# Three output blocks' share of one hidden block moved from TensorE to VectorE, and the low parts of the weights from VectorE to GpSimd

## The chip, the core and the metric

The kernel runs on one core of one Trainium2 chip. A core has TensorE (PE, the matrix unit, which writes to the PSUM banks only), VectorE (DVE), ScalarE (ACT), GpSimd (POOL), SyncE (SP, which here issues nearly all transfers) and 16 DMA engines that all transfers share. Every engine works through its own instructions strictly in their written order; semaphores tie the engines together. The metric is the device time of one execution in microseconds (us), the median of several runs.

## What is computed

The model is one step of a small decoder layer on T = 288 tokens (256 new ones of one prompt and 8 x 4 of samples). What matters here is the last part, the MLP with a width of 8192:

```python
h2 = rmsnorm(x, norm2_g)
f = jnp.square(jax.nn.relu(jnp.einsum("btd,df->btf", h2, w_ff1)))   # 2048 -> 8192
x = x + jnp.einsum("btf,fd->btd", f, w_ff2)                         # 8192 -> 2048
```

Everything before it (a norm, a projection, a convolution group, a pooling group, an output projection `w_out`) takes the first quarter of the time. Inputs, weights and outputs are float32.

## The kernel before

Activations lie transposed, channels on the 128 partitions and the 288 tokens in the free dimension; `xT` holds the residual stream as 16 blocks of 128 channels. TensorE works on rounded 32-bit numbers, so each operand is split into a high part (a cast on ScalarE) and a low part (the difference, a subtraction), and one product of a 128x128 weight block with a 128x288 activation block is three matmuls: high x high, high x low, low x high (`product`, L288 to L293). The three add into the same PSUM bank.

The MLP goes in four chunks of 2048 hidden channels (`FCH`). A chunk has a first half (FF1: 8 groups of two blocks, each summed over the 16 blocks of `xT`) and a second (FF2: 8 groups of two output blocks, each summed over the chunk's 16 hidden blocks). A group is thus 16 x 2 products, 96 matmuls (`gemm`). It goes over the 16 blocks, and inside each over its two PSUM banks, so two banks are in use at a time. There are four such banks (`acc`, bufs=4), so the next group has two banks while the last one's are read out. Two further pools of two banks each (`cvp`, `msp`) serve other uses.

- FF1's read-out: VectorE takes relu and the scale `r2` in one instruction (L584, tile `t`), ScalarE squares (`f`) and casts (`fh`), VectorE subtracts (`fl`, L589).
- FF2's read-out: VectorE adds the bank to `xT` (L600, the function `evict`).
- Weights come as tiles of 128x1024 (`wr`, 512 KB each, six buffers), four to a group. ScalarE casts each to `whi` (L284), and VectorE (GpSimd in the first stages) subtracts to `wlo` (L285). There are four buffers of each, so a tile's cast waits until TensorE has done with the tile four before it. The generator `weight_groups` decides which engine makes which low part; the split of a group stands one group ahead of its matmuls.

The order on each engine is set by a scheduler at build time, which gives each piece of work a place by its estimate of when it can run, work inside `later()` behind all other that is ready. Data dependencies follow the order in which the Python text issues the work: of two instructions that write the same slice of `xT`, the one issued first in the text stays first. When it places a group it also picks the banks, so a bank that is held long is simply not there for the groups after it.

In the stage before the MLP (`w_out`, two halves of 8 groups) the convolution's norm lies between the halves: a token sum (`pt`, L227), a few small VectorE instructions, a transposition back (`pr`, L276), then `n`, `cc`, `mh` per block, and the second half's matmuls read `mh`.

Of the kernel before, what the change touches and what calls it, by code (L numbers as in the profile page):

```python
# [9 lines left out]
F32 = mybir.dt.float32  # L10
F32R = mybir.dt.float32r
AF = mybir.ActivationFunctionType
ALU = mybir.AluOpType
# [3 lines left out]
P = 128  # L17
# [3 lines left out]
T = SEQ + NB * NS  # L21
DC = DP = 1024
DFF = 8192
# [6 lines left out]
N8 = DC // P  # L30
WINDOWS = (2, 4, 8, 16)
FCH = 2048
US = CH + NS
UO = CH + SEQ
UL = UO + NB * US
ZS = PH + NS
# [5 lines left out]

GROUPS = (3, 2, 1, 0)
SEQUENCE = [("conv", i) for i in range(2, 7)] + [("pool", 3), ("pool", 2), ("pool", 1), ("mix", 3), ("pool", 0), ("mix", 2), ("conv", 7)]


def weight_blocks():

    def w_in(*cols):
        return [("w_in", r, cols) for r in range(0, D, 1024)]  # L50

    a, b = [w_in(i * P, DC + i * P) for i in range(2)]
    yield from (a[0], b[0], a[1], b[1])
    for kind, i in SEQUENCE:
        if kind == "mix":
            if i == 3:
                yield "pool_w", 0, (0, P)
            continue
        yield from w_in(i * P, DC + i * P) if kind == "conv" else w_in(2 * DC + 2 * i * P, 2 * DC + (2 * i + 1) * P)
    for r in (DC, 0):  # L60
        for c in range(0, D, 256):
            yield "w_out", r, (c, c + P)
    for ch in range(0, DFF, FCH):
        for c in range(ch, ch + FCH, 256):
            for r in range(0, D, 1024):
                yield "w_ff1", r, (c, c + P)
        for c in range(0, D, 256):
            for r in range(ch, ch + FCH, 1024):
                yield "w_ff2", r, (c, c + P)
# [12 lines left out]
def trunk_kernel(ctx: ExitStack, tc: tile.TileContext, io):  # L82
    nc = tc.nc
# [5 lines left out]
    actp = ctx.enter_context(tc.tile_pool(name="actp", bufs=40))  # L89
    tmpp = ctx.enter_context(tc.tile_pool(name="tmpp", bufs=6))  # L90
    prdp = ctx.enter_context(tc.tile_pool(name="prdp", bufs=1))
    acc = ctx.enter_context(tc.tile_pool(name="acc", bufs=4, space=PSUM))
    cvp = ctx.enter_context(tc.tile_pool(name="cvp", bufs=2, space=PSUM))
    msp = ctx.enter_context(tc.tile_pool(name="msp", bufs=2, space=PSUM))
# [3 lines left out]
    def nm(s):  # L98
        seen[s] = seen.get(s, 0) + 1
        return f"{s}{seen[s]}"  # L100

    @contextmanager
    def later(by=LATER):

        tc.cur_priority += by
        yield
        tc.cur_priority -= by

    def row(name):
        return rowp.tile([P, T], F32, name=nm(name), tag="row")  # L110
# [4 lines left out]
    def act(name, **kw):  # L115
        return slot(name, F32R, **(kw or {"tag": "act"}))
# [13 lines left out]
    def f32(t):  # L130
        return t[:].bitcast(F32)
# [8 lines left out]
    xT = const.tile([P, KT, T], F32, name="xT")  # L140
    uz = const.tile([P, N8 * (UL + ZL)], F32, name="uz")
# [137 lines left out]
    def split(raw, eng, cuts=((0, 4),)):  # L279

        hi = wspl.tile([P, 4, 256], F32R, name=nm("whi"), tag="whi")
        lo = wspl.tile([P, 4, 256], F32R, name=nm("wlo"), tag="wlo")
        for a, b in cuts:
            nc.scalar.copy(hi[:, a:b, :], raw[:, a:b, :])  # L284
            eng.tensor_tensor(lo[:, a:b, :], raw[:, a:b, :], hi[:, a:b, :].bitcast(F32), op=ALU.subtract)  # L285
        return hi, lo

    def product(bank, rhs, w, first, last):  # L288

        (xh, xl), (wh, wl), b = rhs, w, bank[:, :T]  # L290
        nc.tensor.matmul(b, wh, xh, start=first, stop=False)  # L291
        nc.tensor.matmul(b, wh, xl, start=False, stop=False)  # L292
        nc.tensor.matmul(b, wl, xh, start=False, stop=last)  # L293

    def gemm(banks, rhs, m_outer=False, hooks={}):

        n = len(rhs)
        get = ready.pop()
        order = [(k, m) for k in range(n) for m in range(len(banks))]
        if m_outer:  # L300
            order.sort(key=lambda km: km[1])
        for j, (k, m) in enumerate(order):
            hooks.get(j, bool)()
            product(banks[m], rhs[k], get(k, m), k == 0, k == n - 1)
        ready.extend(itertools.islice(weights, 1))

    korder = [2 * g + m for g in GROUPS for m in range(2)]
# [1 line left out]
    def halves(parts, at=lambda k: k):  # L309

        def get(k, m):
            k = at(k)
            return tuple(t[:, k % 4, m * P : (m + 1) * P] for t in parts[k // 4])

        return get

    def weight_groups():

        V, G = nc.vector, nc.gpsimd
        def mix(g):  # L320

            return halves(parts, lambda k: 2 * g + k)

        for kind, i in SEQUENCE:
            if kind == "mix":
                if i == 3:
                    parts = [split(raw, G) for raw in load()]
                yield mix(i)
            else:
                yield halves([split(raw, G) for _ in range(2) for raw in load()])  # L330
        yield mix(1)
        yield mix(0)
        for _ in range(8):
            yield halves([split(raw, G) for raw in load()], lambda k: korder[k])
        for _ in range(8):
            yield halves([split(raw, V) for raw in load()])
        for _ in range(2 * DFF // 256):
            yield halves([split(raw, V) for _ in range(2) for raw in load()])

    weights = weight_groups()  # L340
    ready = []
# [15 lines left out]
    for c in range(8):  # L357
# [5 lines left out]
        for k0, k1 in steps:  # L363
# [174 lines left out]
    for g in range(8):  # L538
        bk = bank2()
# [10 lines left out]
    for g in range(8):  # L550
        bk = bank2()
        gemm(bk, mixc)
        for m in range(2):
            k = 2 * g + m
# [9 lines left out]
            else:  # L564
                q2 = bank("q", cvp, "cv")[:, :T]
                nc.scalar.activation(q2, xk, AF.Square)
                nc.vector.tensor_tensor(ss2, ss2, q2, op=ALU.add)

    r2 = row("r2")
    ss2 = parts(ss2)  # L570
    pss = ms("pss")
# [2 lines left out]
    pf = ms("pf", 8)  # L574
    for ch in range(DFF // FCH):
        fx = []
        for g in range(FCH // 256):
            bk = bank2()
            gemm(bk, x1, hooks={4: lambda: column_sum(pss, ones_r, ss2)} if ch == 0 and g == 0 else {})
            if ch == 0 and g == 0:  # L580
                rsqrt_wide(pss, r2, 1.0 / D)
            for m in range(2):
                t = tmp("t")
                nc.vector.scalar_tensor_tensor(out=t, in0=bk[m][:, :T], scalar=0.0, in1=r2, op0=ALU.max, op1=ALU.mult)  # L584
                f = tmp("f")
                nc.scalar.activation(f, t, AF.Square)
                fh, fl = act("fh"), act("fl")
                nc.scalar.copy(fh, f)
                nc.vector.tensor_tensor(fl, f, f32(fh), op=ALU.subtract)  # L589
                fx.append((fh, fl))  # L590
        last = ch == DFF // FCH - 1
        for g in range(8):
            bk = bank2()

            def evict(m):

                nonlocal last_square
                k = 2 * g + m
                xk = xT[:, k, :]
                nc.vector.tensor_tensor(xk, xk, bk[m][:, :T], op=ALU.add)  # L600
                if last:
                    if k == 0:
                        nc.scalar.activation(ssf, xk, AF.Square)
                    else:
                        qf = tmp("q")
                        nc.scalar.activation(qf, xk, AF.Square)
                        if k < KT - 1:
                            nc.vector.tensor_tensor(ssf, ssf, qf, op=ALU.add)
                        else:
                            busy(ssf, 4)  # L610
                            token_sum(pf, qf, first=False)
                            last_square = qf
                    nc.scalar.activation(xk, xk, AF.Copy, scale=v("norm_f", k))

            if last and g == 7:
                gemm(bk, fx, m_outer=True, hooks={16: lambda: evict(0), 28: lambda: token_sum(pf, ssf, last=False)})
            else:
                gemm(bk, fx)
                evict(0)
            evict(1)  # L620

# [73 lines left out]
```

## Time and profile before

| | |
|---|---|
| median of 3 runs | 1080.83 us (1080.81 to 1081.02) |
| the profiled execution's own time | 1080.9 us |
| its span, as the profile shows it | 1078.8 us |
| PE busy | 1066.5 us, 99% of the span |
| DVE busy | 633.7 us, 59% |
| ACT busy | 471.3 us, 44% |
| POOL busy | 167.4 us, 16% |
| TensorE clock granted | 0.996 of full |

A row of the groups reads: line, engine, operation, written tile `<-` read tiles, shapes, count, then busy time in all and the mean duration of one in ns, then the idle time of that engine in front of it and what ended it. Busy time counts overlapping instructions once, so for instructions that start before the one ahead has ended, it is less than count times mean. A row of the timeline gives the start and the time covered in us, with equal instructions in a row merged (`x11`). The MLP runs from about 266 us to 1065 us, some 200 us a chunk.

### The profile page before, as it was taken

To read this page: it belongs to the slowest core of one execution; us is meant where nothing else is said; L and a number is where in the kernel's file an instruction comes from. 1 tells how busy PE (TensorE), PEld (TensorE's weight loads), DVE (VectorE), ACT (ScalarE), POOL (GpSimd) and SP (SyncE) were. 2 spreads that over 40 slices of the span, in tenths; PEclk is the share of its full clock that TensorE was granted. 3 is DMA by queue.
4 is the path that set the end of the run, shared out by engine and by line. 5 is a ranking of instruction groups with operands and counts; after the bars stand their busy time and mean duration, and the time that the engine had idled before them with its cause. 6 is when DMAs were issued, how large, how long until landed. Compare 5 with 4: busy or idle time off the path is not lost.

```text
span 1078.8 us, 19743 instructions
## 1 busy us (share of the span) xinstructions
PE 1066.5 (99%) x8190; PEld 1065.2 (99%) x8190; DVE 633.7 (59%) x983; ACT 471.3 (44%) x650; POOL 167.4 (16%) x112
## 2 busy tenths in 40 slices
PE   9999999999999999999999999999999999999996
PEld 8999999999999999999999999999999999999996
DVE  7799999687745544445554444455444455554553
ACT  7544554575444433334443333444433334444441
POOL 0899888500000000000000000000000000000001
PEclk9999999999999999999999999999999999999998
DMA  9655567555555555555555555555555555555532
GB/s 335 227 185 176 178 198 215 167 168 165 174 165 168 175 165 169 174 162 173 170 166 173 170 166 174 166 168 176 166 167 173 165 171 169 168 171 166 169 97 88
DMA packets 56937, 187.04 MB, mean 173 GB/s; under 512 B 5904, under 2 KB 11664, under 8 KB 56848
## 3 DMA queue, kind: packets, MB, share of 16 engines
q1 hardware_dynamic: 56416, 185.15, 53.6%
q8 instruction: 64, 1.05, 0.4%
q10 hardware_dynamic: 432, 0.64, 0.2%
q14 instruction: 25, 0.20, 0.1%
HBM read 181.49 MB, written 4.28 MB: 172 GB/s over the span
## 4 chain that ended last, share of the span: by engine, by line
PE 98%; DMA 0%; DVE 0%; ACT 0%; SPq 0%; DVEq 0%; issue 0%
PE ac L292 32%; PE ac L291 32%; PE ac L293 32%; PE ac L380 1%; PE cv L380 1%; DMA xT<-in_xT 0%; DVE xT L627 0%; PE pr L276 0%; PE pf L227 0%; ACT hh L366 0%; SPq L175 0%; SPq L168 0%; DVEq L681 0%; ACT uz L350 0%; PE m L293 0%
## 5 line engine op out<-in xcount | busy, mean ns | idle before, releaser
L284 ACT CAST whi<-wr 128x1024 fp32r<-128x1024 f32 x330 | 344.9, 1046 | 570.3 <-PE ac L292 538.0
L285 DVE TENSOR_TENSOR wlo<-wr,whi 128x1024 fp32r<-128x1024 f32 x272 | 333.4, 1226 | 361.0 <-ACT whi L284 361.0
L291 PE MATMUL ac<-fh,whi 128*128 128x288 f32 x1024 | 298.2, 291 | 0.0
L292 PE MATMUL ac<-al,whi 128*128 128x288 f32 x1024 | 298.1, 291 | 0.0
L293 PE MATMUL ac<-fh,wlo 128*128 128x288 f32 x1024 | 298.1, 291 | 0.0
L291 PE MATMUL ac<-ah,whi 128*128 128x288 f32 x1024 | 298.1, 291 | 0.0
L293 PE MATMUL ac<-ah,wlo 128*128 128x288 f32 x1024 | 298.1, 291 | 0.0
L292 PE MATMUL ac<-fl,whi 128*128 128x288 f32 x1024 | 298.1, 291 | 0.0
L292 PEld LDWEIGHTS ac<-fl,whi 128*128 128x128 f32 x1024 | 191.7, 187 | 0.0
L291 PEld LDWEIGHTS ac<-fh,whi 128*128 128x128 f32 x1024 | 191.7, 187 | 0.0
L292 PEld LDWEIGHTS ac<-al,whi 128*128 128x128 f32 x1024 | 191.7, 187 | 0.0
L291 PEld LDWEIGHTS ac<-ah,whi 128*128 128x128 f32 x1024 | 191.7, 187 | 0.0
L293 PEld LDWEIGHTS ac<-ah,wlo 128*128 128x128 f32 x1024 | 191.7, 187 | 0.0
L293 PEld LDWEIGHTS ac<-fh,wlo 128*128 128x128 f32 x1024 | 191.7, 187 | 0.0
L285 POOL TENSOR_TENSOR wlo<-wr,whi 128x1024 fp32r<-128x1024 f32 x58 | 138.3, 2403 | 20.4 <-ACT whi L284 20.4
L627 POOL TENSOR_TENSOR xT<-xT,rg 128x576 f32<-128x576 f32 x2 | 2.8, 1402 | 798.2 <-ACT rg L632 798.2
L433 DVE SCALAR_TENSOR_TENSOR pc<-uz,vec,pc 128x256 f32<-128x256 f32 x232 | 98.6, 482 | 5.3 <-ACT pc L422 3.5
L292 PE MATMUL ac<-hl,whi 128*128 128x288 f32 x320 | 92.1, 291 | 0.0
L291 PE MATMUL ac<-hh,whi 128*128 128x288 f32 x320 | 92.0, 291 | 0.0
L293 PE MATMUL ac<-hh,wlo 128*128 128x288 f32 x320 | 87.3, 291 | 0.0
L291 PEld LDWEIGHTS ac<-hh,whi 128*128 128x128 f32 x320 | 59.9, 187 | 0.0
L292 PEld LDWEIGHTS ac<-hl,whi 128*128 128x128 f32 x320 | 59.9, 187 | 0.0
(165 smaller groups left out, 934.6 us busy)
## 6 DMA issues: line engine op xcount, KB each, us to landing
wr<-in_w SPq DMA_DIRECT2D x336, 512.0 KB, 3.7
out_u_out<-uz SPq DMA_DIRECT2D x1, 1208.0 KB, 9.6
xT<-in_xT SPq DMA_DIRECT2D x2, 576.0 KB, 8.2
uz<-in_hist_c SPq DMA_DIRECT2D x1, 1088.0 KB, 12.1
wr<-in_w SPq DMA_DIRECT2D x4, 256.0 KB, 5.1
xT<-in_xT SPq DMA_DIRECT2D x3, 288.0 KB, 5.9
out_yT<-xT SPq DMA_DIRECT2D x2, 432.0 KB, 3.5
out_z_out<-uz SPq DMA_DIRECT2D x1, 668.0 KB, 7.5
```

What stands on the lines that cost most here:

```text
L284: nc.scalar.copy(hi[:, a:b, :], raw[:, a:b, :])
L285: eng.tensor_tensor(lo[:, a:b, :], raw[:, a:b, :], hi[:, a:b, :].bitcast(F32), op=ALU.subtract)
L291: nc.tensor.matmul(b, wh, xh, start=first, stop=False)
L292: nc.tensor.matmul(b, wh, xl, start=False, stop=False)
L293: nc.tensor.matmul(b, wl, xh, start=False, stop=last)
L380: nc.tensor.matmul(first_banks[m][:, :T], lhs(w, k, m), pair[k][x], start=c == 0 and k == 0 and w is hi and x == 0, stop=c == 7 and k == 1 ...
L433: nc.vector.scalar_tensor_tensor(out=dst, in0=u_all[:, i, w : w + SEQ], scalar=cw[i][:, w : w + 1], in1=pc[i], op0=ALU.mult, op1=ALU.add)
L627: eng.tensor_tensor(xk, xk, by[:, None, :T].to_broadcast([P, n, T]), op=ALU.mult)
```

## The change

In each of the first three chunks, the chunk's first hidden block (`f` of the first FF1 group, first bank) is no longer multiplied by TensorE for three of the 16 output blocks: blocks 0 to 2 in chunk 0, 3 to 5 in chunk 1, 6 to 8 in chunk 2 (`HELD_BY`, `owned`). For these, `gemm` leaves out the first of the 16 products (`without`). VectorE computes them as 128 rank-one updates per output block, in full float32: hidden channel k's row of 288 tokens, copied to all partitions, times the column of 128 weights for k, added to a sum in PSUM (L618 for k = 0, L620 for the rest). To bring a row to all partitions, `f` is written to DRAM (L606, tile `fd`, 144 KB) and read back four rows at a time, each partition reading the same 4608 bytes (L611, 32 reads of 576 KB per chunk, four buffers in `uz`). The weight blocks are loaded once more and transposed ahead of the MLP, in the `w_out` stage (`turn`: 36 small transfers, L595, and 9 VectorE transpositions, L599). The sums of a chunk lie in three banks of the pools `cvp` and `msp`; at the end VectorE adds them to `xT` (L622). All of it is issued inside `later()`, and in the text right behind the first `f`, ahead of the chunk's `evict` calls.

In the first three chunks GpSimd, not VectorE, makes the low parts of the weights and of `f` (now L293 and L648); in the last chunk VectorE makes them as before. Other line numbers have grown too: read-out of FF1 is now L641, `evict`'s addition L659, the three matmuls L299 to L301.

```diff
+HELD_BY = (3, 3, 3)
+ROWS, HELD = 4, 4
...
+    held = ctx.enter_context(tc.tile_pool(name="held", bufs=2, space=bass.MemoryType.DRAM))
...
-        order = [(k, m) for k in range(n) for m in range(len(banks))]
+        order = [(k, m) for k in range(n) for m in range(len(banks)) if k or m not in without]
...
-            product(banks[m], rhs[k], get(k, m), k == 0, k == n - 1)
+            product(banks[m], rhs[k], get(k, m), k == int(m in without), k == n - 1)
...
-        for _ in range(2 * DFF // 256):
-            yield halves([split(raw, V) for _ in range(2) for raw in load()])
+        for ch in range(DFF // FCH):
+            for _ in range(16):
+                yield halves([split(raw, G if ch < len(HELD_BY) else V) for _ in range(2) for raw in load()])
...
+    def turn():
+
+        with later():
+            for ch in range(len(HELD_BY)):
+                for m in owned(ch):
+                    src = io["w"][ff2_blocks(ch)[m // 2]][:, 0, (m % 2) * P : (m % 2 + 1) * P]
+                    for j in range(4):
+                        nc.sync.dma_start(
+                            blocks[32 * j : 32 * j + 32, m, :].rearrange("r (i c) -> r i c", c=32),
+                            src[:, 32 * j : 32 * j + 32].rearrange("(i r) c -> r i c", r=32),
+                        )
+                    nc.vector.transpose(turned[:, m, :], blocks[:, m, :])
...
+    def own_products(ch, f):
+
+        fd = held.tile([P, T], F32, name=nm("fd"), tag="fd")
+        nc.sync.dma_start(fd, f)
+        with later():
+            part = {m: bank("own", cvp, "cv") if j < 2 else ms("own") for j, m in enumerate(owned(ch))}
+            for b in range(P // ROWS):
+                at = rows_all[:, next(held_at) % HELD]
+                nc.sync.dma_start(at, fd[b * ROWS : (b + 1) * ROWS, :].partition_broadcast(P))
+                for r in range(ROWS):
+                    k = b * ROWS + r
+                    for m in owned(ch):
+                        to = part[m][:, :T]
+                        by = turned[:, m, k : k + 1]
+                        if k == 0:
+                            nc.vector.tensor_scalar(to, at[:, r, :], by, None, op0=ALU.mult)
+                        else:
+                            nc.vector.scalar_tensor_tensor(out=to, in0=at[:, r, :], scalar=by, in1=to, op0=ALU.mult, op1=ALU.add)
+            for m in owned(ch):
+                nc.vector.tensor_tensor(xT[:, m, :], xT[:, m, :], part[m][:, :T], op=ALU.add)
...
+                if g == 0 and m == 0 and owned(ch):
+                    own_products(ch, f)
                 fh, fl = act("fh"), act("fl")
                 nc.scalar.copy(fh, f)
-                nc.vector.tensor_tensor(fl, f, f32(fh), op=ALU.subtract)
+                (nc.gpsimd if ch < len(HELD_BY) else nc.vector).tensor_tensor(fl, f, f32(fh), op=ALU.subtract)
...
-                gemm(bk, fx)
+                gemm(bk, fx, without=[m for m in range(2) if 2 * g + m in owned(ch)])
                 evict(0)
             evict(1)
```

The diff does not show how the order moves. Three places matter.

The first is VectorE at the end of chunk 0's FF2. The names `ac_...` are the PSUM sums of output blocks; 5159, 5160 and 5277 are those of the three blocks that VectorE shares in (0, 1 and 2), 5278 that of block 3, and 5398, 5399, 5522, ... 5895, 6018, 6019 those of blocks 4 to 15.

```order
L659 TENSOR_TENSOR xT<-xT,ac_5895 128x288
L620 SCALAR_TENSOR_TENSOR own_3759<-uz,own_3759 128x288
L620 SCALAR_TENSOR_TENSOR own_3760<-uz,own_3760 128x288
L620 SCALAR_TENSOR_TENSOR own_3761<-uz,own_3761 128x288
L622 TENSOR_TENSOR xT<-xT,own_3759 128x288
L622 TENSOR_TENSOR xT<-xT,own_3760 128x288
L622 TENSOR_TENSOR xT<-xT,own_3761 128x288
L659 TENSOR_TENSOR xT<-xT,ac_5159 128x288
L659 TENSOR_TENSOR xT<-xT,ac_5160 128x288
L659 TENSOR_TENSOR xT<-xT,ac_5277 128x288
L659 TENSOR_TENSOR xT<-xT,ac_6018 128x288
L659 TENSOR_TENSOR xT<-xT,ac_6019 128x288
```

The read-outs of blocks 0, 1 and 2, whose sums TensorE has finished first of all, now stand behind VectorE's last own product and its additions to `xT` (L622), since the text issues those additions first. Between every two read-outs from block 3's to block 13's (ac_5278 to ac_5895, eleven read-outs, ten gaps) stand 17 rows of L620. Chunk 1 has seven such gaps (its blocks 7 to 13, behind ac_8033, block 6) and chunk 2 five (blocks 10 to 14, behind ac_10672, block 9).

Before, the same stretch of VectorE had read-outs in pairs, each pair between low parts of weights:

```order
L285 TENSOR_TENSOR wlo_4803<-wr_4798,whi_4802 128x1024
L600 TENSOR_TENSOR xT<-xT,ac_4688 128x288
L600 TENSOR_TENSOR xT<-xT,ac_4689 128x288
L285 TENSOR_TENSOR wlo_4807<-wr_4800,whi_4806 128x1024
L285 TENSOR_TENSOR wlo_4915<-wr_4910,whi_4914 128x1024
L285 TENSOR_TENSOR wlo_4919<-wr_4912,whi_4918 128x1024
L285 TENSOR_TENSOR wlo_4927<-wr_4922,whi_4926 128x1024
L600 TENSOR_TENSOR xT<-xT,ac_4812 128x288
L600 TENSOR_TENSOR xT<-xT,ac_4813 128x288
```

The second place is TensorE in the same stretch, where block 4's sum ends and block 5's begins:

```order
L299 MATMUL ac_5398<-fh_5155,whi_5392 128x288
L300 MATMUL ac_5398<-fl_5156,whi_5392 128x288
L301 MATMUL ac_5398<-fh_5155,wlo_5393 128x288
L299 MATMUL ac_5399<-fh_4181,whi_5376 128x288
L300 MATMUL ac_5399<-fl_4182,whi_5376 128x288
L301 MATMUL ac_5399<-fh_4181,wlo_5377 128x288
```

All 48 matmuls of one output block now stand together and the other block of its group behind them. In the built program the sums 5278, 5398, 5399 and so on to 5895 and 6018 lie in one and the same bank, while 5159, 5160 and 5277 hold the other three of the four; each block's first matmul waits for the read-out of the block before it. Before, the two blocks of a group alternated after every three matmuls, in two banks:

```order
L291 MATMUL ac_5060<-fh_4124,whi_5042 128x288
L292 MATMUL ac_5060<-fl_4125,whi_5042 128x288
L293 MATMUL ac_5060<-fh_4124,wlo_5043 128x288
L291 MATMUL ac_5061<-fh_4124,whi_5042 128x288
L292 MATMUL ac_5061<-fl_4125,whi_5042 128x288
L293 MATMUL ac_5061<-fh_4124,wlo_5043 128x288
```

The third place is SP's queue, where in chunk 0 the writing of `f` and the first reads of its rows have come in between the weight loads:

```order
L168 DMA wr_4431<-in_w 128x1024
L606 DMA fd_3757<-f_3755 128x288
L168 DMA wr_4441<-in_w 128x1024
L611 DMA uz<-fd_3757 128x1152 x4
L168 DMA wr_4443<-in_w 128x1024
L168 DMA wr_4567<-in_w 128x1024
L168 DMA wr_4569<-in_w 128x1024
L611 DMA uz<-fd_3757 128x1152
```

From there on one L611 stands behind every two to four weight loads; from the fifth on, each waits until VectorE has done with the buffer it writes.

More of the change, by code (lines that the diff above doesn't have):

```diff
@@ L44, with ff2_blocks @@
 SEQUENCE = [("conv", i) for i in range(2, 7)] + [("pool", 3), ("pool", 2), ("pool", 1), ("mix", 3), ("pool", 0), ("mix", 2), ("conv", 7)]
+def ff2_blocks(ch):
+    return [j for j, b in enumerate(weight_blocks()) if b[0] == "w_ff2" and b[1] == ch * FCH]
 def weight_blocks():
@@ L293, in product, with gemm @@
         nc.tensor.matmul(b, wl, xh, start=False, stop=last)
-    def gemm(banks, rhs, m_outer=False, hooks={}):
+    def gemm(banks, rhs, m_outer=False, hooks={}, without=()):
         n = len(rhs)
         get = ready.pop()
-        order = [(k, m) for k in range(n) for m in range(len(banks))]
+        order = [(k, m) for k in range(n) for m in range(len(banks)) if k or m not in without]
         if m_outer:
@@ L567, in trunk_kernel, with owned @@
                 nc.vector.tensor_tensor(ss2, ss2, q2, op=ALU.add)
+    own = sum(HELD_BY)
+    turned = uz[:, 0 : own * P].rearrange("p (m k) -> p m k", k=P)
+    blocks = uz[:, own * P : 2 * own * P].rearrange("p (m k) -> p m k", k=P)
+    rows_all = uz[:, 2 * own * P : 2 * own * P + HELD * ROWS * T].rearrange("p (h r t) -> p h r t", h=HELD, t=T)
+    def owned(ch):
+        first = sum(HELD_BY[:ch])
+        return range(first, first + (HELD_BY[ch] if ch < len(HELD_BY) else 0))
+    def turn():
[9 more added lines that the diff above has]
+                    nc.vector.transpose(turned[:, m, :], blocks[:, m, :])
+    held_at = itertools.count()
+    def own_products(ch, f):
[17 more added lines that the diff above has]
+                nc.vector.tensor_tensor(xT[:, m, :], xT[:, m, :], part[m][:, :T], op=ALU.add)
+    turn()
     r2 = row("r2")
```

## The prediction, made before the run

> **What bounds the kernel now.** I read the busy times and the chain of waits first. Both say TensorE:
>
> ```profile
> PE 1066.5 (99%) x8190; PEld 1065.2 (99%) x8190; DVE 633.7 (59%) x983; ACT 471.3 (44%) x650; POOL 167.4 (16%) x112
> ...
> PE 98%; DMA 0%; DVE 0%; ACT 0%; SPq 0%; DVEq 0%; issue 0%
> ```
>
> A "busy" PE need not be at its peak, so I took its pace from the windows, here one half chunk of FF1 and one of FF2 (columns: window, length, then busy us and matmul count of PE, PEld, DVE, ACT, POOL, clock, DMA share, GB/s):
>
> ```profile
> core 0: us, PE busy (x) PEld busy (x) DVE busy (x) ACT busy (x) POOL busy (x), PEclk, DMA share, GB/s
> 265.70:365.60 99.90, 99.90 (x771) 99.90 (x770) 57.53 (x71) 46.13 (x66) 2.10 (x2) 1.00 0.53 169
> 365.60:465.50 99.90, 99.90 (x771) 99.90 (x770) 46.73 (x50) 34.81 (x36) 0.00 (x0) 1.00 0.53 169
> ```
>
> 771 matmuls in 99.90 us is one each 0.1296 us, at full clock and with no gap: a group of 96 takes 12.44 us, the 48 of one output block 6.22. So time falls by less TensorE work and rises by any wait that TensorE is given. VectorE and GpSimd have room; the price is in who waits.
>
> **What the change takes off TensorE.** Three blocks x three chunks x one product of three matmuls: 27 x 0.1296 = 3.5 us. This is the only gain.
>
> **What an own product costs.** The trace has no such instruction, but the convolution's taps (L433) have its form: one SBUF tensor, a scalar column, a sum in PSUM read and written.
>
> ```profile
> L433 DVE SCALAR_TENSOR_TENSOR pc<-uz,vec,pc 128x256 f32<-128x256 f32 x232 | 98.6, 482 | 5.3 <-ACT pc L422 3.5 <-POOL wlo L285 1.5
> ...
> 63.40 4.40 DVE L433 SCALAR_TENSOR_TENSOR pc<-uz,vec,pc 128x256 f32<-128x256 f32 x11
> 67.71 0.87 DVE L433 SCALAR_TENSOR_TENSOR c<-uz,vec,pc 128x256 f32<-128x256 f32 x2
> ...
> L285 DVE TENSOR_TENSOR wlo<-wr,whi 128x1024 fp32r<-128x1024 f32 x272 | 333.4, 1226 | 361.0 <-ACT whi L284 361.0
> L589 DVE TENSOR_TENSOR fl<-f,fh 128x288 fp32r<-128x288 f32 x64 | 26.3, 453 | 0.0
> ```
>
> Each lasts 482 ns, but eleven start in 67.71 - 63.40 = 4.31 us, one each 0.392: neighbours overlap. That is for 256 columns; L285 against L589 gives (1226 - 453)/(1024 - 288) = 1.05 ns a column, so 288 columns take 0.392 + 0.034 = 0.426 us. The taps' two sums alternate, the own products' three do, so the dependence is no tighter. The upper end is no overlap at all, 0.482 + 0.034 = 0.516; the lower is 0.392.
>
> **FF1 with the change.** About 26 own products stand between two groups' read-outs. They and the two L641 fill 26 x 0.426 + 2 x 0.39 = 11.9 us of a group's 12.44: VectorE keeps up, by 0.6 us, and the product runs free behind TensorE. GpSimd's new work per group is four tiles and two `fl`:
>
> ```profile
> L285 POOL TENSOR_TENSOR wlo<-wr,whi 128x1024 fp32r<-128x1024 f32 x58 | 138.3, 2403 | 20.4 <-ACT whi L284 20.4
> L438 POOL TENSOR_TENSOR sum_c<-sum_c,c 128x288 f32<-128x288 f32 x7 | 5.7, 812 | 0.0
> ```
>
> 4 x 2.40 + 2 x 0.81 = 11.2 us, again inside 12.44; these 58 ran beside the taps, so the company is the same. Cost nothing while TensorE covers both.
>
> **FF2 with the change, the main term.** Behind block 3 of chunk 0 (6 and 9 in the others) three of the four banks are held until the own sums are done, and TensorE goes block by block through one bank. Each block must wait for the read-out of the one before. What that is, where VectorE is free:
>
> ```profile
> 377.93 0.29 PE L293 MATMUL ac<-fh,wlo 128*128 128x288 f32 x1
> ...
> 378.26 0.84 DVE L600 TENSOR_TENSOR xT<-xT,ac 128x288 f32<-128x288 f32 x2 [0.56 <-PE ac L293]
> ...
> L600 DVE TENSOR_TENSOR xT<-xT,ac 128x288 f32<-128x288 f32 x64 | 27.1, 455 | 25.7 <-PE ac L293 25.7
> ```
>
> The read-out starts 0.33 after the last matmul's start, lasts 0.455, and for the signal back I take the 0.04 that passed there from the matmul's end (377.93 + 0.29) to VectorE's start; the next matmul would have come after 0.13, so TensorE stands 0.33 + 0.455 + 0.04 - 0.13 = 0.70 us. But VectorE is not free: 17 own products lie between read-outs. Its period is 17 x 0.426 + one read-out at 0.84 - 0.455 = 0.385 of spacing, together 7.63 us, against TensorE's 6.22 + 0.70 = 6.92. VectorE is the slower and sets the pace, and TensorE loses 7.63 - 6.22 = 1.41 us a block. There are 10 + 7 + 5 = 22 such blocks: 31.0 us; the first waiting block of each chunk loses 0.70: 2.1. Ahead of these stretches own products do not block (49 of them, 20.9 us, beside two groups of 90 and 93 matmuls, 23.7 us). At the stretches' ends block 14 or 15 gets a freed bank while the other block runs. GpSimd sets a third pace: a tile's last reader now stands in the group's second block, the first tile is free 1.6 us into it, and cast (1.05) plus four low parts (9.6) must be there when the next group's fourth quarter begins, which asks for a period of some 7.45 us. It lies just under VectorE's. Sum here: +33.1 us. Lower end with 0.392: period 7.05, 22 x 0.83 + 2.1 = +20.4.
>
> **The own rows' transfers.** Per chunk 32 reads of 576 KB come onto the 16 DMA engines, beside 64 tiles of 512 KB:
>
> ```profile
> wr<-in_w SPq DMA_DIRECT2D x336, 512.0 KB, 3.7
> ...
> out_u_out<-uz SPq DMA_DIRECT2D x1, 1208.0 KB, 9.6
> out_yT<-xT SPq DMA_DIRECT2D x2, 144.0 KB, 1.8
> ```
>
> 32 tiles take 53% of 99.90 us, 1.65 us each; by bytes a row load takes 1.86. Per FF1 group: 4 x 1.65 + 26/12 x 1.86 = 10.6 of 12.44 us. That fits. The upper bound is out_u_out's 1208 KB in 9.6 us beside the weights, 4.6 us for a row load; the limit is (12.44 - 6.6)/2.17 = 2.7. I take 1.86, whose row has the nearest shape. SP, too, waits: an L611 that finds VectorE late holds the weight loads behind it. Four buffers of rows are 48 products, 20 us ahead, and six weight tiles 18 us, so I cost it at nothing; the `fd` write (144 KB, 1.8 us as out_yT) delays only the start.
>
> **The stage before.** Nine transpositions, 36 transfers and the weight loads behind them lie beside the taps. `pr` now stands 22 rows later on TensorE, directly ahead of the first `mh` products:
>
> ```profile
> 212.16 0.80 PE L276 MATMUL pr<-ident,st 96*128 96x96 f32 x6
> ...
> 213.01 0.46 DVE L530 TENSOR_TENSOR n<-c,pr 128x288 f32<-128x288 f32 x1 [1.21 <-PE pr L276]
> ...
> 214.16 0.43 ACT L534 CAST mh<-cc 128x288 fp32r<-128x288 f32 x1
> ```
>
> `mh` is there 214.59 - 212.16 = 2.43 us after `pr` begins, TensorE is done with `pr` after 0.80: it stands 1.6 us that other matmuls covered before. I take +1.6 (0 if it is covered, 5 if the transpositions hold up the taps).
>
> **The sum.** -3.5 + 33.1 + 1.6 = +31.2. The profiled execution took 1080.9 us (span 1078.8), the median of the runs is 1080.83, so the same: 1112 us.
>
> **Rivals.**
>
> *The banks' wait alone (or GpSimd) sets the pace, VectorE being quicker than 0.426.* For it: 0.392 is measured, at 256 columns. With 0.70 at all 25 blocks: 17.5 - 3.5 + 0 = 1095; with GpSimd's 7.45, 22 x 1.23 + 2.1 - 3.5 + 1.6 = 1108. 14 in 100, most of it near 1108.
>
> *The row loads become the bound.* 128 partitions read the same 4608 bytes; no row of the trace reads one address so often. Should a load take twice 1.86, 3.7 us, an FF1 group takes 6.6 + 2.17 x 3.7 = 14.6, +2.2 on 21 groups = 46, and two one-bank blocks (34 products) 6.6 + 2.83 x 3.7 = 17.1 against 15.3, +1.8 on 11 pairs = 20: 1178 us. It decides from 2.7 us a load. Against it: the DMA share is 0.53 now. 11 in 100. The Trainium skill, "DMA: Bandwidth & Descriptors", section "Latency and other measured facts", reports that 128 partitions' streams with one large power-of-two pitch fall to about half their rate, and takes channel aliasing for the cause; one address for all would be that case or a worse one, and by that rule the time is this rival's.
>
> *Own products do not overlap, 0.516 us.* An FF1 group takes 26 x 0.516 + 2 x 0.455 = 14.3 (+1.9 on 21), a one-bank block 17 x 0.516 + 0.455 = 9.2 (+3.0 on 22): 40 + 66 + 2 - 3.5 + 1.6 = +106, 1187 us. Against it are the eleven taps above. 6 in 100.
>
> *Faster.* The own sums end before the one-bank stretch begins, so the held banks come free, all waits go and 3.5 us come off: 1077. Place and price are the main term's. It decides where the 384 products of a chunk fit between the first rows (some 24 us into the chunk) and the end of block 3's sum (99.9 + 23.7 = 123.6 us): 0.26 us each, against 0.392 as the least the trace shows. 3 in 100, and 2 in 100 that it ends within 0.2%.
>
> **Chances and range.** Forecast 64 in 100, with a range of its own of 1103 to 1125 (0.40 to 0.45 us a product, 0 to 5 before). A measurement of this kernel can tell about 0.2% from no change. Together: slower 0.95, same 0.02, faster 0.03. The range 1095 to 1150 takes in the pace of the banks alone and slightly late row loads, not the two rivals near 1180.
>
> **What would show it.** Right: L620 at a spacing of 0.42 to 0.43; in chunk 0's FF2 read-outs 7.6 us apart and a PE gap of 1.4 us in front of each block from 4 to 14; none in FF1; chunks 0, 1, 2 longer by about 15, 11 and 8 us, less 1.2 each; chunk 3 unchanged; no PE idle that a transfer ends. Wrong: L620 spaced 0.5 or idle behind L611 (a rival above); PE gaps in FF1; a POOL tile over 2.5 us, which would lift the third pace over VectorE's; or one-bank blocks without gaps. A gap over 2 us in front of the `mh` products would say that the first stage is mis-sized.

## The result, and the profile after

The changed kernel takes 1115.1 us (1113.7 to 1115.5) against 1081.0 us before; the ratio is 1.0313, with a 95% interval of 1.0301 to 1.0324. So it is slower by 34 us, where 1112 us had been forecast. One execution, the profiled one of that set, was disturbed as a whole (6102.7 us, a matmul 1120 ns instead of 291) and is left out; the profile shown here is from a second set of the same kernel (median 1114.05 us, profiled execution 1114.55 us, span 1112.7 us).

The page of it: busy times, PE's busy tenths in 40 slices, the chain that ended last by engine, and the own products' group:

```profile
PE 1071.5 (96%) x8163; PEld 1064.3 (96%) x8163; DVE 877.6 (79%) x1913; ACT 475.6 (43%) x650; POOL 660.1 (59%) x352
...
PE   9999999899999988899999989999999899999996
...
PE 82%; DVE 15%; issue 1%; ACT 1%; POOL 0%; DMA 0%; SPq 0%; DVEq 0%; POOLq 0%; ACTq 0%
...
L620 DVE SCALAR_TENSOR_TENSOR own<-uz,own 128x288 f32<-128x288 f32 x1143 | 492.7, 514 | 0.0
```

Before, TensorE was at 9 in every slice but the last and held 98% of the chain. Now there are dips in four places, one ahead of the MLP and three in it, and VectorE holds 15% of the chain. The waits of TensorE say for whom (engine, line, whom it waited for, us in total, times, longest):

```profile
PE ac L299 <- DVE xT L659: 25.8, 25, 1.2
PE ac L299 <- ACT mh L543: 1.7, 1, 1.7
...
PE ac L301 <- POOL wlo L293: 1.3, 1, 1.3
```

25 waits for FF2's read-outs, the number of the blocks that wait in the forecast. None waits for a transfer. The windows put them in place: FF1 and FF2 of chunks 0, 1 and 2, the changed kernel first, then the kernel before (columns as in the prediction).

```profile
271.09:371.21 100.12, 100.12 (x772) 100.12 (x771) 83.32 (x186) 47.69 (x66) 88.39 (x49) 1.00 0.79 264
371.21:484.25 113.04, 101.59 (x761) 99.17 (x760) 102.81 (x245) 35.06 (x36) 75.56 (x35) 1.00 0.68 228
484.25:584.09 99.84, 99.84 (x770) 99.84 (x769) 76.72 (x183) 43.94 (x60) 88.74 (x48) 1.00 0.82 273
584.09:693.11 109.02, 100.70 (x761) 98.99 (x760) 100.33 (x238) 35.06 (x36) 74.39 (x34) 1.00 0.69 232
...
792.95:899.20 106.25, 100.22 (x762) 98.93 (x760) 103.48 (x243) 35.13 (x36) 71.27 (x32) 1.00 0.73 241
```

```profile
265.86:365.97 100.11, 100.11 (x772) 100.11 (x771) 57.56 (x72) 46.13 (x66) 2.10 (x2) 1.00 0.53 169
365.97:465.81 99.84, 99.84 (x770) 99.84 (x769) 46.73 (x51) 34.81 (x36) 0.00 (x0) 1.00 0.53 169
```

FF1 has not moved by more than 0.01 us. FF2 has grown by 13.20, 9.18 and 6.41 us, and the MLP begins at 271.09 instead of 265.86, 5.23 us late. Together 34.0 us; the spans differ by 33.9. Nothing else is left to explain.

### The profile page after: what moved, and what is told of

It is laid out like the page before. It is cut to its first block, busy times and chain, and to the rows that moved or that the text cites. A ratio compares the mean times of both kernels' runs of the same rounds, so it can differ in the third digit from the quotient of the medians.

```text
span 6100.9 us, 21196 instructions
## 1 busy us (share of the span) xinstructions
PE 6074.0 (100%) x8163; PEld 6049.1 (99%) x8163; DVE 886.4 (15%) x1913; ACT 475.5 (8%) x650; POOL 652.5 (11%) x352
## 4 chain that ended last, share of the span: by engine, by line
PE 100%; DVE 0%; issue 0%; ACT 0%; DVEq 0%
PE ac L299 32%; PE ac L301 32%; PE ac L300 32%; PE ac L389 1%; PE cv L389 1%; PE warm L223 0%; DVE xT L659 0%; PE pr L284 0%; PE idle L264 0%; PE pf L235 0%; DVE xT L686 0%; PE m L300 0%; PE pmean L520 0%; PE m L299 0%; PE m L301 0%
## 5 line engine op out<-in xcount | busy, mean ns | idle before, releaser
L299 PE MATMUL ac<-fh,whi 128*128 128x288 f32 x1015 | 1147.3, 1130 | 14.8 <-DVE xT L659 14.8
L300 PE MATMUL ac<-al,whi 128*128 128x288 f32 x1024 | 1147.0, 1120 | 0.0
L299 PE MATMUL ac<-ah,whi 128*128 128x288 f32 x1024 | 1146.3, 1119 | 0.0
L301 PE MATMUL ac<-ah,wlo 128*128 128x288 f32 x1024 | 1145.4, 1120 | 0.0
L300 PE MATMUL ac<-fl,whi 128*128 128x288 f32 x1015 | 1139.3, 1122 | 0.0
L301 PE MATMUL ac<-fh,wlo 128*128 128x288 f32 x1015 | 1139.1, 1123 | 0.0
L293 POOL TENSOR_TENSOR wlo<-wr,whi 128x1024 fp32r<-128x1024 f32 x250 | 587.8, 2351 | 4154.8 <-ACT whi L292 4137.2
L299 PEld LDWEIGHTS ac<-fh,whi 128*128 128x128 f32 x1015 | 925.6, 912 | 38.0 <-ACT whi L292 20.1
L300 PEld LDWEIGHTS ac<-al,whi 128*128 128x128 f32 x1024 | 936.9, 915 | 0.0
L299 PEld LDWEIGHTS ac<-ah,whi 128*128 128x128 f32 x1024 | 936.5, 915 | 0.0
L301 PEld LDWEIGHTS ac<-ah,wlo 128*128 128x128 f32 x1024 | 936.0, 915 | 0.0
L301 PEld LDWEIGHTS ac<-fh,wlo 128*128 128x128 f32 x1015 | 933.4, 920 | 0.0
L620 DVE SCALAR_TENSOR_TENSOR own<-uz,own 128x288 f32<-128x288 f32 x1143 | 492.8, 515 | 0.0
L299 PE MATMUL ac<-hh,whi 128*128 128x288 f32 x320 | 358.5, 1120 | 0.0
L301 PE MATMUL ac<-hh,wlo 128*128 128x288 f32 x320 | 345.1, 1121 | 0.0
L299 PEld LDWEIGHTS ac<-hh,whi 128*128 128x128 f32 x320 | 293.0, 916 | 0.0
L301 PEld LDWEIGHTS ac<-hh,wlo 128*128 128x128 f32 x320 | 286.6, 915 | 0.0
L659 DVE TENSOR_TENSOR xT<-xT,ac 128x288 f32<-128x288 f32 x64 | 28.6, 453 | 1575.7 <-PE ac L301 1575.7
```

The source lines that it names most:

```text
L620: nc.vector.scalar_tensor_tensor(out=to, in0=at[:, r, :], scalar=by, in1=to, op0=ALU.mult, op1=ALU.add)
```

## The experiments

The table has each kernel's median and, read from its timeline, where the first matmul of the MLP stands and how long FF2 lasts from its first matmul to the next chunk's. FF1 takes 99.84 us in every kernel (some 100.1 in chunk 0). The kernel before was timed beside each set, at 1080.94 to 1080.99 us; a ratio is to those runs.

| run | edit | median, us | MLP begins | FF2 of chunks 0, 1, 2 |
|---|---|---|---|---|
| before | | 1080.99 | 265.86 | 99.84, 99.84, 99.84 |
| e0_after | the change | 1114.05 | 271.09 | 113.04, 109.02, 106.25 |
| e1_late_add | L622 issued behind FF2 | 1081.69 | 270.13 | 98.67, 98.67, 98.67 |
| e2_low_parts | low parts on GpSimd alone | 1080.75 | 265.89 | 99.84, 99.84, 99.84 |
| e3_few_rows | 4 of 32 row loads | 1114.47 | 270.99 | 113.04, 109.00, 106.24 |
| e4_turn_only | `turn` alone | 1085.17 | 271.74 | 99.84, 99.84, 99.84 |
| e5_turn_mlp | e1, `turn` tied to the MLP's start | 1077.13 | 265.83 | 98.67, 98.67, 98.66 |
| e6_half_k | own products of even k only | 1082.05 | 268.90 | 99.56, 98.67, 98.67 |
| e7_two_blocks | two blocks a chunk | 1084.57 | 270.55 | 100.03, 99.55, 99.06 |
| e8_turn_dma | `turn`'s transfers alone | 1081.17 | 266.16 | 99.84, 99.84, 99.84 |

### The changed kernel again, for its trace

> The changed kernel itself, for its trace. Main theory (the bank held by the order of the text, VectorE's pace): own products (L620) 0.42 to 0.43 us apart; in chunk 0's FF2 the read-outs of blocks 3 to 13 are 7.6 us apart with a TensorE gap of some 1.4 us before each block; no gap in FF1; chunks 0, 1, 2 take about 214, 210, 207 us instead of some 200, chunk 3 as before; a gap of some 1.6 us ahead of the first mh products. Rival (bank wait alone): read-outs 6.9 us apart. Rival (GpSimd's pace): 7.45 us apart, TensorE waiting for wlo. Rival (row loads): gaps in FF1 too, VectorE idle behind L611.

Its median was 1114.05 us (ratio 1.0308, 1.0292 to 1.0323). VectorE in chunk 0's FF2, from the timeline:

```profile
395.20 0.45 DVE L659 TENSOR_TENSOR xT<-xT,ac 128x288 f32<-128x288 f32 x1 [1.18 <-PE ac L301]
395.57 7.32 DVE L620 SCALAR_TENSOR_TENSOR own<-uz,own 128x288 f32<-128x288 f32 x17
402.80 0.44 DVE L659 TENSOR_TENSOR xT<-xT,ac 128x288 f32<-128x288 f32 x1
403.17 7.31 DVE L620 SCALAR_TENSOR_TENSOR own<-uz,own 128x288 f32<-128x288 f32 x17
410.39 0.44 DVE L659 TENSOR_TENSOR xT<-xT,ac 128x288 f32<-128x288 f32 x1
```

Only the first read-out has a bracket, a time in which VectorE waited for TensorE. From there on VectorE never stands, and the read-outs are 7.59 us apart (410.39 - 402.80). TensorE in front of the first waiting block, at that block's end, and around the last of these read-outs (matmuls in between are left out at `...`):

```profile
394.87 0.29 PE L301 MATMUL ac<-fh,wlo 128*128 128x288 f32 x1
395.80 0.37 PE L299 MATMUL ac<-fh,whi 128*128 128x288 f32 x1 [0.64 <-DVE xT L659]
...
402.00 0.29 PE L301 MATMUL ac<-fh,wlo 128*128 128x288 f32 x1
...
409.52 0.29 PE L301 MATMUL ac<-fh,wlo 128*128 128x288 f32 x1
410.98 0.37 PE L299 MATMUL ac<-fh,whi 128*128 128x288 f32 x1 [1.16 <-DVE xT L659]
```

The step from one block's last matmul to the next block's first is 1.46 us here instead of 0.13, and 1.20 to 1.31 at every second block. The matmul at 409.52 begins 0.87 us before the read-out at 410.39; with VectorE free, at 394.87, it was 0.33. So the wait has two parts. The bank alone costs some 0.9 us, as at the first waiting block, where VectorE was free: its last matmul, at 402.00, comes 7.13 us after the one at 394.87, and 48 matmuls without a wait take 6.24 (99.84 us for the 768 of a half chunk). The rest is VectorE's queue of own products, which reaches the read-out 0.54 us late. With the bank's wait alone the read-outs would stand some 7.1 us apart.

The profile puts 11 of the 25 waits of the weight loads at these places (15.1 us) down to ScalarE, whose fourth cast of the group ends within 0.04 us of the read-out. That cast is not what TensorE waits for: block 4 began at 395.80 while the cast of its own group's fourth tile was still running (395.12 to 396.17).

GpSimd was near its limit in this stretch, though not over it. Its four tiles of a group:

```profile
436.56 9.46 POOL L293 TENSOR_TENSOR wlo<-wr,whi 128x1024 fp32r<-128x1024 f32 x4 [5.44 <-ACT whi L292]
```

They end at 446.02. The group that needs them is the one whose first block begins after the read-out at 440.75, and the matmul that first reads the fourth tile begins at 446.35, 0.3 us later: the tile comes just in time. Had VectorE been much quicker, GpSimd would have set the pace next, at the 7.45 us of the forecast or near it. This wasn't tried by itself.

### The additions moved behind FF2

In the text, the three additions L622 are issued after the chunk's FF2 groups instead of ahead of them. The own products, the rows and the low parts are the same.

```diff
-            for m in owned(ch):
-                nc.vector.tensor_tensor(xT[:, m, :], xT[:, m, :], part[m][:, :T], op=ALU.add)
+        return part
+
+    def add_own(ch, part):
+
+        with later():
+            for m in owned(ch):
+                nc.vector.tensor_tensor(xT[:, m, :], xT[:, m, :], part[m][:, :T], op=ALU.add)
...
             evict(1)
+        if owned(ch):
+            add_own(ch, part)
```

> The same work; only the three additions L622 are issued in the text behind the chunk's FF2 groups, so that no read-out has to wait for the own sums and no bank is held. Main theory: the 33 us of bank waits go, 1080.9 - 3.5 + 1.6 = 1079 us, at most 1081; own products still 0.42 us apart, TensorE without gaps in the chunks. Rival (row loads, or VectorE or GpSimd too slow for the work as such): it stays above 1095 us, with the gaps in other places.

It takes 1081.69 us (1080.49 to 1083.58), 1.0009 (1.0000 to 1.0019) of before. FF2 of chunk 0:

```profile
370.25:468.92 98.67, 98.67 (x761) 98.67 (x760) 93.42 (x221) 35.07 (x36) 78.08 (x35) 1.00 0.81 269
```

TensorE has no gap and the nine left out matmuls come off (99.84 - 1.17). VectorE is as busy as before the edit, 93.42 of 98.67 us (102.81 of 113.04 there), and is in nobody's way, since its read-outs come in their usual pairs. So all of the 28.8 us of FF2 (32.3 without the matmuls that come off) came from the order in which two additions to the same slice of `xT` were issued, and none from the own products as work. What is left of the loss lies ahead of the MLP: 4.27 us.

### The low parts alone

```diff
-        for _ in range(2 * DFF // 256):
-            yield halves([split(raw, V) for _ in range(2) for raw in load()])
+        for ch in range(DFF // FCH):
+            for _ in range(16):
+                yield halves([split(raw, G if ch < 3 else V) for _ in range(2) for raw in load()])
...
-                nc.vector.tensor_tensor(fl, f, f32(fh), op=ALU.subtract)
+                (nc.gpsimd if ch < 3 else nc.vector).tensor_tensor(fl, f, f32(fh), op=ALU.subtract)
```

> The kernel before with the low parts alone moved to GpSimd (weights and f of the first three chunks); no own products, no leaving out. Main theory: 11.2 us of GpSimd per group of 12.44, so nothing is lost: 1081 us, within 2 us. Rival (GpSimd is a bound of its own): some 0.5 us or more for each of 48 groups, 1105 us or more.

1080.75 us, 0.9998 (0.9989 to 1.0007) of before. This half of the change costs nothing:

```profile
L285 POOL TENSOR_TENSOR wlo<-wr,whi 128x1024 fp32r<-128x1024 f32 x250 | 598.9, 2407 | 172.6 <-ACT whi L284 172.5
```

A tile takes GpSimd 2.41 us, as in the first stages, and its idle time ends with ScalarE's cast, as it should where TensorE leads.

### Most of the row loads left out

```diff
-                nc.sync.dma_start(at, fd[b * ROWS : (b + 1) * ROWS, :].partition_broadcast(P))
+                if b < HELD:
+                    nc.sync.dma_start(at, fd[b * ROWS : (b + 1) * ROWS, :].partition_broadcast(P))
```

> The changed kernel with 4 of each chunk's 32 row loads; the other 28 are left out, and the own products read rows that are there already, so the sums of the nine blocks are not the reference's. Order on TensorE, VectorE and GpSimd is the same. Main theory: the row loads fit, so the time stays at that of the changed kernel, 1115 us within 3. Rival (row loads hold up VectorE or the weights): 1100 us or less.

1114.47 us (ratio 1.031, 1.0293 to 1.0327), and FF2 to within 0.02 us what it was: the row loads are not in the way. The two pages give their price too, the first from the changed kernel, the second from this one (queue, packets, MB, share of 16 engines):

```profile
q1 hardware_dynamic: 75856, 242.81, 65.9%
```

```profile
q1 hardware_dynamic: 63760, 193.26, 53.2%
```

0.659 x 1112.7 - 0.532 x 1112.9 = 141 us for 84 loads, 1.68 us each: less than the 1.86 by bytes, and 576 KB in the time of a 512 KB weight tile (1.65). The Trainium skill's rule of the prediction, "DMA: Bandwidth & Descriptors", section "Latency and other measured facts", that streams with one large power-of-two pitch fall to half their rate, does not carry over to 128 partitions that read one address: these loads ran at full rate.

### Half of the own products

```diff
                     k = b * ROWS + r
                     for m in owned(ch):
+                        if k % 2:
+                            continue
```

> The changed kernel, L622 where it was, with the own products of odd k left out (192 per chunk; the nine sums lack them). Theory (the bank is held as long as own products are outstanding in FF2): the own sums end near FF2's first groups, no one-bank blocks are left, at most a wait or two of 0.7 to 1.2 us per chunk: 1080.9 - 3.5 + 5.2 = 1082.6 us, at most 1088. Rival (the loss is from own products as such, or from GpSimd): half of the 29 us or more stays, above 1095 us.

1082.05 us (1.0013, 1.0004 to 1.0022). With L622 in its old place, one wait of 0.6 us is left in chunk 0. The own products now end 19 to 21 us into FF2, before its second pair of blocks is done, so the banks are free in time; the one wait left comes of the additions' place behind block 3's read-out in chunk 0. The loss is not in proportion to the own products: half of them cost FF2 0.9 us in place of 32 (28.8 and the 3.5 that come off). It must begin somewhere between the two, which agrees with where the prediction put its faster rival: own products still outstanding when FF2's first four blocks are done.

### Two blocks instead of three

```diff
-HELD_BY = (3, 3, 3)
+HELD_BY = (2, 2, 2)
```

> The changed kernel with two blocks per chunk instead of three (HELD_BY 2, 2, 2), L622 where it was. Two of four banks are then held until the additions, and two are left, so TensorE keeps its pairs. Theory (it is the one bank that serializes, and VectorE's 17 products per read-out): each of the one to three pairs per chunk that run without spare banks waits for read-outs, 0.7 to 1.2 us: 1080.9 - 2.3 + 5 + some 5 = 1088 us, 1083 to 1093. Rival (the loss goes with the number of own products): two thirds of 29 us stay, 1103 us.

1084.57 us (1.003, 1.0018 to 1.0042), near the lower end of what was expected. Two banks stay free, TensorE keeps its pairs, and these are all its waits for read-outs:

```profile
PE ac L299 <- DVE xT L659: 0.7, 3, 0.2
```

Without any wait FF2 would take 99.84 - 2 x 3 x 0.13 = 99.06; it takes 1.0, 0.5 and 0.0 us more. The own products are two thirds, the loss in FF2 is 1.5 us in place of 32.3: it is the third bank that makes it large. Not all of the difference is the bank's, since with fewer products the own sums also end earlier, at 416.0 us in chunk 0 against 472.8. But the 45 us of FF2 up to there, more than three pairs of blocks, cost 1.0 us here, where each single block lost 1.35 in the changed kernel. What else is lost here, 4.7 us, lies ahead of the MLP.

### `turn` alone

The kernel before, with `turn` (its 36 transfers and 9 transpositions, called where the change calls it) and nothing else:

```diff
+    turn()
+
     r2 = row("r2")
```

> The kernel before plus turn alone (36 transfers, 9 transpositions ahead of the MLP, their result unused). Theory now (the transpositions wait on VectorE for their transfers and hold the convolution's taps behind them, in the changed kernel by 7.3 us at the last tap): the MLP begins some 5 us later, 1086 us, the chunks as before. Theory of the prediction (only pr's place on TensorE costs): +1.6, 1082.5 us, the last tap at most 2.7 us later (the nine transpositions themselves).

1085.17 us (1.004, 1.0027 to 1.0054). The MLP begins 5.88 us late and the chunks are as before, so the whole of the loss ahead of the MLP is `turn`'s. On VectorE, among the taps (L440 here):

```profile
172.38 1.26 DVE L440 SCALAR_TENSOR_TENSOR pc<-uz,vec,pc 128x256 f32<-128x256 f32 x3
177.97 0.31 DVE L597 STREAM_TRANSPOSE uz<-uz 128x128 f32<-128x128 f32 x1 [4.32 <-DMA uz<-in_w]
178.20 2.02 DVE L440 SCALAR_TENSOR_TENSOR pc<-uz,vec,pc 128x256 f32<-128x256 f32 x5
181.34 0.31 DVE L597 STREAM_TRANSPOSE uz<-uz 128x128 f32<-128x128 f32 x1 [1.13 <-DMA uz<-in_w]
```

VectorE stands 4.32 us at the first transposition, which waits for its transfer, and the taps stand behind it. In the waits of SP's queue of this kernel is the reason that the transfer is late:

```profile
SPq L593 <- DMA out_u_out<-uz: 7.4, 1, 7.4
```

The blocks are loaded into `uz`, over the convolution's input, whose copy to the output (`out_u_out`, 1208 KB) is still being read from there. SP stands 7.4 us until it is done, a wait that the order's place for the transpositions did not allow for. In the changed kernel the same wait is 7.2 us, and the last tap starts at 199.14 instead of 191.83.

What this costs TensorE is seen in the steps between its matmuls. In the changed kernel's trace three places make up 4.9 of the 5.23 us. In the first, GpSimd stands until a tap's result is there, and a low part of the weights behind it comes late: TensorE waits for it at 195.87, a step of 1.55 us instead of 0.13 (1.4 lost). The second is the gap between `pr` and the first `mh` product that the prediction named, 1.95 instead of 0.13 (1.8 lost). The third is the stretch behind that gap, with 16 matmuls in 3.75 us (1.7 lost). GpSimd, TensorE, and the window of the third place (the clock is the third number from the end):

```profile
194.22 0.81 POOL L447 TENSOR_TENSOR sum_c<-sum_c,c 128x288 f32<-128x288 f32 x1 [4.43 <-DVE c L442]
```

```profile
197.42 0.40 PE L301 MATMUL ac<-ph,wlo 128*128 128x288 f32 x1 [1.26 <-POOL wlo L293]
...
217.03 0.80 PE L284 MATMUL pr<-ident,st 96*128 96x96 f32 x6
219.50 1.15 PE L299 MATMUL ac<-mh,whi 128*128 128x288 f32 x4 [1.67 <-ACT mh L543]
```

```profile
219.50:223.25 3.75, 3.75 (x16) 3.75 (x17) 3.43 (x9) 3.36 (x8) 0.00 (x0) 0.54 0.40 140
```

The granted clock was 0.54 there, and 1.00 in the windows on both sides. The norm's own lateness is in none of the three: `pr` follows the matmul ahead of it (216.90) without a gap. The `mh` wait of 1.67 us is the same in every trace with transpositions in this stage, but the slow stretch behind it is not: 15 to 18 matmuls in the changed kernel, with few row loads, with `turn` alone and with two blocks, but three (0.3 us) with the late additions and with half of the products. This is a good part of why the loss ahead of the MLP is anywhere from 3.0 to 5.9 us in the table. What decides the length of the stretch is not shown.

### `turn`'s transfers without the transpositions

```diff
-                    nc.vector.transpose(turned[:, m, :], blocks[:, m, :])
```

> The kernel before plus turn's 36 transfers alone, without the nine transpositions (the blocks are loaded and not used). Orders of TensorE, VectorE and GpSimd are those of the kernel before, SP's is that of turn alone (1085.2 us). Theory (VectorE stands at the transpositions until their transfers land, and the taps behind it): 1081 us, the MLP beginning at 266 to 267. Rival (the 36 transfers on SP's queue delay the weights of the w_out stage): 1084 us or more, with TensorE waiting for wlo.

1081.17 us (1.0001, 0.9991 to 1.0010), the MLP begins at 266.16. SP waits 7.5 us for `out_u_out` here too, and nobody is hurt. So it is not the transfers that cost the 3 to 6 us ahead of the MLP, nor the weights behind them on SP, but the nine transpositions. They do it in two ways that this run removes together. VectorE stands at them, which holds up the taps and GpSimd's low part; and with them the scheduler puts `pr` directly ahead of the first `mh` product, whereas here, as in the kernel before, 23 other matmuls lie between. By the trace above the first way costs 1.4 us and the second 3.5.

### A version that is faster than both

The additions moved as above, and `turn` tied to the end of the `w_out` stage by a small copy that its transfers must wait for:

```diff
     def turn():
 
+        nc.vector.tensor_copy(blocks[:, :, 0:1], ss2[:, 0:own].rearrange("p (m o) -> p m o", o=1))
         with later():
```

> The late-addition kernel with turn tied to the end of the w_out stage (one small copy from the sum of squares into the buffer, which the transfers must wait for). Theory now: the 4.3 us in front of the MLP go and the 3.5 us of left out matmuls stay: 1077.4 us, MLP beginning at 265.9, FF2 of chunks 0 to 2 at 98.7 us. Rival (the small transfers now hold up weights or first rows inside chunk 0): gaps in chunk 0, 1080 us or more.

1077.13 us (1076.69 to 1077.49), 0.9965 (0.9953 to 0.9978) of before: the 3.5 us of left out matmuls, and a little more. Its transpositions still wait 18 us in all for their transfers, but between 274 and 298 us, in the MLP's first groups, and TensorE waits for none of it. Page and one window:

```profile
PE 1063.9 (99%) x8163; PEld 1062.7 (99%) x8163; DVE 878.3 (82%) x1914; ACT 475.5 (44%) x650; POOL 662.2 (62%) x352
```

```profile
365.95:464.62 98.67, 98.67 (x762) 98.67 (x761) 95.31 (x227) 35.06 (x36) 79.14 (x35) 1.00 0.83 278
```

## Why the prediction was right, point by point

- **The gain, -3.5 us.** Right. Where no bank was waited for, FF2 took 98.67 us instead of 99.84, 1.17 in each of three chunks.
- **The own product, 0.426 us.** Right. 17 of them and one read-out take 7.59 us; with 0.37 from the read-out's start to the next product's (403.17 - 402.80) each takes 0.425. An instruction lasts 514 ns, 2 ns under the upper end of the forecast, but neighbours overlap as the taps do.
- **FF1 without loss.** Right, to 0.01 us. VectorE is busy 83 and 77 us of some 100, GpSimd 88 (`fl` included).
- **FF2, one bank, VectorE's pace.** Right in mechanism, place and size: +28.8 us net where 33.1 - 3.5 = 29.6 was forecast; read-outs 7.59 us apart (7.63), 25 waiting blocks (25), chunks +13.2, +9.2, +6.4 (13.6, 9.4, 6.6 by the forecast's terms). A waiting block loses 1.35, not 1.41, and the first of each chunk, which waits for the bank alone, some 0.86, not 0.70: 22 x 1.35 + 3 x 0.86 = 32.3, and the two errors partly cancel. The 0.70 left out that the next matmul begins 0.06 to 0.15 us after the read-out's end, not 0.04, and that one more step behind it is some 0.1 longer. A pace of 0.1296 us a matmul was also read a little low, because the window's 771 takes in matmuls that only touch its edges; 768 in 99.84 us are 0.130 each, 6.24 a block. That the order of the text is the cause, and not VectorE's load, is shown by the moved additions; that it takes the third held bank, in the main, by the kernel with two.
- **Row loads.** Right: hidden, and 1.68 us each where 1.86 was taken. SP's wait behind L611 (96 us in 74 waits for own products) did not reach TensorE, as costed.
- **The stage before, +1.6 us.** Wrong in size: 5.2 us, a little over the upper bound of 5 that was given. The `mh` gap itself was there and as forecast (1.8 us). Two terms were put at nothing. One is the slower stretch behind the gap, 16 matmuls at a granted clock of 0.54, 1.7 us. The other comes from the step "nine transpositions, 36 transfers and the weight loads behind them lie beside the taps", which looked at their durations and not at what they wait for. The transfers had to wait for `out_u_out`, whose 9.6 us stood in the prediction's own rows; the transpositions for the transfers; the taps for the transpositions, in order; GpSimd for a tap, and TensorE for GpSimd's low part, 1.4 us. The last tap came 7.3 us late, and TensorE, which had other matmuls to do, felt only that much of it.
- **The sum.** +31.2 forecast, +34.0 in the spans: -0.8 in FF2, +3.6 in the stage before. 1112 us against 1115.1. Most of the error is the stage before.
- **The rivals.** Bank or GpSimd alone: VectorE set the pace, with GpSimd close behind. Row loads as the bound: refuted. No overlap: refuted by 0.425. Faster: its condition was shown with half the products, and its end with the moved additions.

## What to carry to other kernels

When work is moved to an engine that has room, look at what is queued behind it rather than at its load: here some 490 us of new VectorE work cost nothing, and three additions a chunk, issued too early in the text, cost 32 us, because they kept three of four PSUM banks from being read out. A partial sum that is computed on the side should be added where it is ready, behind the read-outs that do not need it. And a transfer into a buffer that is used again begins only when its last reader is done, an output copy included; an instruction on a busy in-order engine that waits for such a transfer holds everything behind it. Where a forecast prices a gap on TensorE, the granted clock behind the gap has to be looked at too: here it cost as much again.

## What was not expected of the hardware

With GpSimd at the low parts earlier, at the end of the `w_out` stage, three of the 16 instructions of one kind on VectorE took over 2 us, where the others took 0.51. The changed kernel, VectorE first, then GpSimd:

```profile
261.74 0.52 DVE L569 SCALAR_TENSOR_TENSOR al<-xT,vec,ah 128x288 fp32r<-128x288 f32 x1
266.48 2.32 DVE L569 SCALAR_TENSOR_TENSOR al<-xT,vec,ah 128x288 fp32r<-128x288 f32 x1 [0.98 <-ACT ah L568]
269.64 2.33 DVE L569 SCALAR_TENSOR_TENSOR al<-xT,vec,ah 128x288 fp32r<-128x288 f32 x1
```

```profile
266.09 2.40 POOL L293 TENSOR_TENSOR wlo<-wr,whi 128x1024 fp32r<-128x1024 f32 x1 [0.67 <-ACT whi L292]
269.26 2.40 POOL L293 TENSOR_TENSOR wlo<-wr,whi 128x1024 fp32r<-128x1024 f32 x1 [0.77 <-DVE ss L576]
```

Both long ones shown begin inside a GpSimd tile and end 0.31 us after it (268.80 and 271.97 against 268.49 and 271.66), as if they had waited for the tile. Their operands `xT` and `ah` both lie in SBUF. The own products read one operand from SBUF and one from PSUM, and were not slowed beside GpSimd: 514 ns on average, both for the 879 that began while a GpSimd instruction ran and for the 264 that did not. The Trainium skill, "SBUF — State Buffer", section "Who interferes with whom", has this rule: a VectorE instruction with two SBUF inputs contends with a GpSimd instruction that reads SBUF, for ports that they share under an exclusive lock; one with a single SBUF input does not, outside modes that use both ports. The trace agrees, with 1.8 us for each of the two shown. In this kernel it cost nothing, since TensorE did not wait for it; had the own sums lain in SBUF, by that rule each own product would have contended with GpSimd's tiles, which was not tried.
